# SwiGLU over 8192 rows on one core: loads and stores on one DMA queue in four-row groups, against two-row tiles with the stores on ScalarE's queue

## The chip, the cores and the metric

One of the eight cores of a Trainium2 chip runs the kernel. The metric is the device time of one execution in microseconds (us). Three runs of the kernel before took 938.91, 939.05 and 939.8 us, median 939.05.

A core has five engines that run programs of their own: PE (TensorE, not used here), DVE (VectorE), ACT (ScalarE), POOL (GpSimd) and SP (SyncE, which here only issues DMA transfers). Sixteen DMA engines move data between the main memory (HBM) and the on-chip buffer (SBUF, 128 partitions).

## The reference

The input has 8192 rows of 8192 float32 numbers. Each row has a left half `a` and a right half `b` of 4096 numbers:

```python
a, b = np.split(x, 2, axis=-1)
silu_b = b / (1 + np.exp(-b))
return a * silu_b
```

So 268.44 MB are read, 134.22 MB are written, and each number of the output costs one SiLU and one product.

## The kernel before, in words

There are three buffers, `slot0` to `slot2`, each with 64 KiB in each of the 128 partitions. That is all the room there is: work flows through these three.

The rows go in 16 groups of 512. A partition takes four neighbouring rows of a group. A group is loaded by two transfers (`load`, L61), each with two rows in each partition: 64 KiB in one piece per partition, 8.39 MB in all. Group g has a slot `keep[g]` for its first two rows and a slot `thru[g]` for the other two (L51 to L54). `swiglu` (L72, L74) runs SiLU on ACT in place on `b`, and then the product on DVE. For the first two rows there is one pair of instructions over 128x8192, for the other two a pair of 128x4096 for each row. The products of all four rows are written side by side into `keep[g]`, over numbers that are no longer needed, so that `store` (L81) writes the group in one transfer of 64 KiB per partition.

All transfers are issued by SP, on one queue, in the order that the loop of L88 to L100 writes out: the loads of group g+1 ahead of the store of group g.

```python
load(g + 1, 0)
load(g + 1, 1)
store(g)
```

`load(g + 1, 0)` goes into the slot that the second half of group g has just left, and waits for DVE's last product. `load(g + 1, 1)` goes into the slot from which group g-1 was stored, and waits until that store has landed. `store(g)` waits for DVE's last product of group g. Each engine works through its own instructions in order, so whatever stands behind a waiting instruction waits too.

The kernel writes its schedule by hand: `behind` (L39) tells the framework which of the earlier instructions on a slot a new one has to wait for, and that the others are ordered already.

Of the kernel before, what the change touches and what calls it, by code (L numbers as in the profile page):

```python
# [1 line left out]

# [4 lines left out]

_SILU = mybir.ActivationFunctionType.Silu


@with_exitstack
def kernel(
    ctx: ExitStack,
    tc: tile.TileContext,
    x: bass.AP,
    out: bass.AP,
):

    nc = tc.nc
    N, M = x.shape
    half = M // 2
    P = nc.NUM_PARTITIONS
    R = 4
    ngroups = N // (P * R)

    xv = x.tensor.reshape([N // R, R * M]).ap()  # L30
    ov = out.tensor.reshape([N // R, R * half]).ap()

    pool = ctx.enter_context(tc.tile_pool(name="sbuf", bufs=1))
    ctx.enter_context(tc.manual_schedule())
    slots = [pool.tile([P, 2 * M], x.dtype, name=f"slot{s}") for s in range(3)]
    touched = [[] for _ in slots]
    newest = {}

    def behind(inst, of, *targets):  # L39


        for s in of:
            for t in touched[s]:
                if t not in targets and t is not newest.get(inst.ins.engine):
                    tc.declare_no_dep(inst.ins, t.ins, reason="ordered by the other waits")
        for s in of:
            touched[s].append(inst)
        newest[inst.ins.engine] = inst
        return inst

    keep, thru = [0, 2], [1, 1]  # L51
    for g in range(2, ngroups):
        keep.append(thru[g - 1])
        thru.append(keep[g - 2])  # L54
    free = {}
    landed = {}
    last = {}

    def load(g, second):
        s = (thru if second else keep)[g]  # L60
        inst = nc.sync.dma_start(  # L61
            out=slots[s], in_=xv[g * P : (g + 1) * P, second * 2 * M : (second + 1) * 2 * M]
        )
        behind(inst, [s], *([free[s]] if s in free else []))
        landed[g, second] = inst

    def swiglu(g, second, k0, k1):
        s, o = (thru if second else keep)[g], keep[g]
        rows = slots[s].rearrange("p (k s c) -> p k s c", k=2, s=2)
        a, b = rows[:, k0:k1, 0], rows[:, k0:k1, 1]  # L70
        to = slots[o].rearrange("p (k c) -> p k c", k=R)[:, 2 * second + k0 : 2 * second + k1]
        gate = nc.scalar.activation(out=b, in_=b, func=_SILU)  # L72
        behind(gate, [s], landed[g, second])
        prod = nc.vector.tensor_mul(out=to, in0=a, in1=b)  # L74
        behind(prod, {s, o}, gate, *([last[g]] if g in last else []))
        last[g] = prod
        free[s] = prod

    def store(g):
        s = keep[g]  # L80
        inst = nc.sync.dma_start(out=ov[g * P : (g + 1) * P], in_=slots[s])  # L81
        behind(inst, [s], last[g])
        free[s] = inst

    load(0, 0)
    load(0, 1)
    load(1, 0)
    for g in range(ngroups):  # L88
        swiglu(g, 0, 0, 2)
        for k in range(2):  # L90
            swiglu(g, 1, k, k + 1)
        if g == 0:
            load(1, 1)
            store(0)
        elif g + 1 < ngroups:
            load(g + 1, 0)
            load(g + 1, 1)
            store(g)
        else:
            store(g)  # L100


# [1 line left out]
_INS = ['x']  # L104
_OUTS = [((8192, 4096), 'float32')]


# [23 lines left out]
```

## Time and profile before

| what | value |
|---|---|
| median of three runs | 939.05 us |
| span of the profiled execution, first to last instruction | 936.2 us |
| DMA queue of SP, share of 16 engines' span | 99.6% |
| moved | 402.67 MB, mean 430 GB/s |
| DVE busy | 279.2 us, 48 products |
| ACT busy | 227.7 us, 48 SiLUs and a table load |
| ACT, 128x8192 / 128x4096 | 7.03 / 3.61 us each |
| DVE, 128x8192 / 128x4096 | 8.69 / 4.42 us each |
| ACT waited for loads | 675.5 us |
| DVE waited for ACT | 629.9 us |

The profile gives the span of its one execution and no separate time for it; 936.2 us stand beside the 938.91 to 939.8 us of the three runs.

The page gives busy time for each engine, and then the span in 40 slices, where each digit is a busy share in tenths. The DMA row is the mean over the 16 DMA engines. The chain of waits follows the work back from the last instruction: at each step to what released it. "Another core or an unknown queue" in it is time for which the profile names no releaser. A timeline row has the start in us, the time that it took, engine, line and operation, output and input with their shapes, and in brackets how long the engine was idle before it and what ended that. A DMA transfer is split over the 16 DMA engines, and on each into packets; here a packet is the 64 KiB of one partition, eight packets for each transfer and engine. The trace has a record of each packet with its start, duration and size.

### The profile page before, as it was taken

What the parts mean: (1) busy time and instruction counts of PE and PEld (TensorE: products, weight loads), DVE (VectorE), ACT (ScalarE), POOL (GpSimd) and SP (SyncE); (2) the same over time, 40 slices, a digit from 0 to 9 for tenths busy, and PEclk for the clock granted to TensorE, in tenths of its full rate; (3) what the DMA queues carried; (4) which work ended last, traced back from release to release, by engine and by line L of the source; (5) the groups of instructions that cost most, each with busy time, mean ns of one, the idle gap of its engine ahead of it and who ended that gap; (6) DMA issues with size and microseconds to landing.
All of it is one profiled execution on the core that took longest, in us unless ns stands there. A gap on an engine that the chain in (4) does not pass through costs nothing.

```text
span 936.2 us, 235 instructions
## 1 busy us (share of the span) xinstructions
DVE 279.2 (30%) x48; ACT 227.7 (24%) x49; POOL 0.2 (0%) x4
## 2 busy tenths in 40 slices
DVE  0446033060330603316033160331503315033250
ACT  0433032330323303233032330413304133041330
POOL 0000000000000000000000000000000000000000
DMA  9999999999999999999999999999999999999997
GB/s 403 448 428 423 423 428 448 431 420 448 426 426 445 428 426 437 440 423 437 440 420 440 440 426 431 442 428 423 448 442 414 442 442 417 440 440 412 448 437 344
DMA packets 6914, 402.67 MB, mean 430 GB/s; under 512 B 768, under 2 KB 768, under 8 KB 768
## 3 DMA queue, kind: packets, MB, share of 16 engines
q1 hardware_dynamic: 6912, 402.66, 99.6%
q14 instruction: 2, 0.02, 0.0%
HBM read 268.44 MB, written 134.22 MB: 430 GB/s over the span
## 4 chain that ended last, share of the span: by engine, by line
DMA 67%; DVE 14%; another core or an unknown queue 9%; ACT 6%; SPq 1%; DVEq 0%; issue 0%
DMA slot<-in_x_dram 62%; DVE slot L74 14%; ACT slot L72 6%; DMA out_dram<-slot 5%; SPq L61 1%; DVEq L126 0%
## 5 line engine op out<-in xcount | busy, mean ns | idle before, releaser
L74 DVE TENSOR_TENSOR slot<-slot 128x4096 f32<-128x4096 f32 (+1 forms) x48 | 279.2, 5845 | 629.9 <-ACT slot L72 629.9
L72 ACT ACTIVATE slot<-slot 128x4096 f32<-128x4096 f32 (+1 forms) x48 | 226.4, 4748 | 675.5 <-DMA slot<-in_x_dram 675.5
L72 ACT ACT_TABLE_LOAD x1 | 1.3, 1283 | 0.7 <-PEq L115 0.7
L115 POOL MEMSET const-bfloat16-1.0<- 128x1 bf16 x1 | 0.1, 102 | 0.0
L115 POOL MEMSET const-uint8-127<- 128x1 uint8 x1 | 0.1, 102 | 0.0
L115 POOL MEMSET const-float32-0.0<- 128x1 f32 x1 | 0.1, 99 | 0.2 <-issue 0.2
L115 POOL MEMSET const-float32-1.0<- 128x1 f32 x1 | 0.1, 99 | 0.0
## 6 DMA issues: line engine op xcount, KB each, us to landing
slot<-in_x_dram SPq DMA_DIRECT2D x32, 32.8
out_dram<-slot SPq DMA_DIRECT2D x16, 57.7
```

The costliest lines, as they stand in the source:

```text
L61: inst = nc.sync.dma_start(out=slots[s], in_=xv[g * P : (g + 1) * P, second * 2 * M : (second + 1) * 2 * M])
L72: gate = nc.scalar.activation(out=b, in_=b, func=_SILU)
L74: prod = nc.vector.tensor_mul(out=to, in0=a, in1=b)
L115: nc = _bacc.Bacc("TRN2", target_bir_lowering=False, num_devices=1)
```

## The change

The slots stay. What flows through them is cut in another way:

- The rows go in 33 tiles: the first and the last have one row in each partition (128 rows, 4.19 MB to load), the 31 between have two (256 rows, 8.39 MB). Tile i has slot i mod 3, for its input and its products.
- A load still is 64 KiB per partition (32 KiB for the two one-row tiles), and still is issued by SP. `load(i + 3)` waits until the store of tile i has landed.
- A store is 32 KiB per partition (16 KiB for the one-row tiles). Stores 0 to 29 are issued by ACT, on its own queue, each right behind the tile's SiLU; of these, 17 and 19 are issued by POOL. Stores 30, 31 and 32 are issued by SP, behind the last load.
- SiLU and product run over both rows at once (128x8192), except in tile 0 (two pieces of 128x2048), tile 31 (row by row) and tile 32 (its one row).

On the engines: DVE has 35 products for 48, ACT 35 SiLUs and 28 stores for 48 SiLUs, POOL two stores, SP 33 loads and 3 stores for 32 loads and 16 stores.

The core of the diff:

```diff
-    R = 4
-    ngroups = N // (P * R)
+    rows = [1] + [2] * (N // (2 * P) - 1) + [1]
+    first = [P * sum(rows[:i]) for i in range(len(rows))]
+    last = len(rows) - 1
...
+    def load(i):
+        s, r = i % 3, rows[i]
+        src = x[first[i] : first[i] + P * r].rearrange("(p r) m -> p (r m)", r=r)
+        inst = nc.sync.dma_start(out=slots[s][:, : r * M], in_=src)
+        behind(inst, s, *([stored[i - 3]] if i >= 3 else []))
+        landed[i] = inst
...
+    def swiglu(i, k0, k1, c0, c1):
+        s, r = i % 3, rows[i]
+        v = slots[s][:, : r * M].rearrange("p (k s c) -> p k s c", k=r, s=2)
+        to = slots[s][:, : r * half].rearrange("p (k c) -> p k c", k=r)
+        b = v[:, k0:k1, 1, c0:c1]
+        gate = nc.scalar.activation(out=b, in_=b, func=_SILU)
+        behind(gate, s, landed[i])
+        prod = nc.vector.tensor_mul(out=to[:, k0:k1, c0:c1], in0=v[:, k0:k1, 0, c0:c1], in1=b)
+        behind(prod, s, gate, *([made[i]] if i in made else []))
+        made[i] = prod
...
+    def store(i, engine):
+        s, r = i % 3, rows[i]
+        dst = out[first[i] : first[i] + P * r].rearrange("(p r) m -> p (r m)", r=r)
+        inst = engine.dma_start(out=dst, in_=slots[s][:, : r * half])
+        behind(inst, s, made[i])
+        stored[i] = inst
...
-    for g in range(ngroups):
-        swiglu(g, 0, 0, 2)
-        for k in range(2):
-            swiglu(g, 1, k, k + 1)
-        if g == 0:
-            load(1, 1)
-            store(0)
-        elif g + 1 < ngroups:
-            load(g + 1, 0)
-            load(g + 1, 1)
-            store(g)
+    for i in range(3):
+        load(i)
+    for i in range(last + 1):
+        if i == 0:
+            swiglu(i, 0, 1, 0, half // 2)
+            swiglu(i, 0, 1, half // 2, half)
+        elif i == last - 1:
+            swiglu(i, 0, 1, 0, half)
+            swiglu(i, 1, 2, 0, half)
         else:
-            store(g)
+            swiglu(i, 0, rows[i], 0, half)
+        if i < last - 2:
+            store(i, nc.gpsimd if i in (17, 19) else nc.scalar)
+            load(i + 3)
+        else:
+            store(i, nc.sync)
```

More of the change, by code (lines that the diff above doesn't have):

```diff
@@ L26 @@
     P = nc.NUM_PARTITIONS
-    R = 4
-    ngroups = N // (P * R)
-    xv = x.tensor.reshape([N // R, R * M]).ap()
-    ov = out.tensor.reshape([N // R, R * half]).ap()
+    rows = [1] + [2] * (N // (2 * P) - 1) + [1]
+    first = [P * sum(rows[:i]) for i in range(len(rows))]
+    last = len(rows) - 1
     pool = ctx.enter_context(tc.tile_pool(name="sbuf", bufs=1))
@@ L37, with behind @@
     newest = {}
[L39 to L47, printed above, removed]
+    landed, made, stored = {}, {}, {}
+    def behind(inst, s, *targets):
+        for t in touched[s]:
+            if t not in targets and t is not newest.get(inst.ins.engine):
+                tc.declare_no_dep(inst.ins, t.ins, reason="ordered by the other waits")
+        touched[s].append(inst)
@@ L48, in behind @@
         newest[inst.ins.engine] = inst
         return inst
[L51 to L87, printed above, removed]
-    for g in range(ngroups):
-        swiglu(g, 0, 0, 2)
-        for k in range(2):
-            swiglu(g, 1, k, k + 1)
-        if g == 0:
-            load(1, 1)
-            store(0)
-        elif g + 1 < ngroups:
-            load(g + 1, 0)
-            load(g + 1, 1)
-            store(g)
-        else:
-            store(g)
+    def load(i):
[4 more added lines that the diff above has]
+        landed[i] = inst
```

## The prediction

> **What bounds the kernel now.** I read the page first: the engines' busy shares, the digits of the slices, the queues. Then the chain of waits, then the timeline, and last the records of single DMA packets.
>
> ```profile
> DVE 279.2 (30%) x48; ACT 227.7 (24%) x49; POOL 0.2 (0%) x4
> ...
> DMA  9999999999999999999999999999999999999997
> ...
> q1 hardware_dynamic: 6912, 402.66, 99.6%
> ```
>
> No engine is busy a third of the span, while the one DMA queue fills 99.6% of it, 9 in every slice but the last. So the kernel is bound by moving 402.66 MB, and waits on ACT, DVE or SP matter only where they leave the DMA engines nothing to do. The chain shows no such place:
>
> ```profile
> 609.68 8.77 DVE slot L74 x2
> 618.45 0.02 issue
> 618.47 0.33 SPq L61
> 618.80 6.57 another core or an unknown queue
> 625.37 0.02 issue
> 625.39 38.61 DMA slot<-in_x_dram
> ```
>
> The 6.57 us are the rest of the store before: the load issued at 618.47 is queued behind it. A transfer is always in the queue.
>
> The packet records give the price of the stream. Each of the 16 DMA engines moves 384 packets of 64 KiB. A packet is recorded with 2418 ns (the median; records overlap by about 4 ns, so 2414 ns from start to start), load or store alike. For one engine, on the mean: first packet at 1.86, 0.76 more on the first packet, 384 x 2.414 = 926.98, 47 borders between transfers at about 6 ns = 0.27, 2.53 at switches from load to store, 0.28 elsewhere: 932.7 us. The records end at 932.8 on the mean and at 935.02 on the slowest engine, 2.24 later; 0.38 more to the landing and 0.81 to the end of the span make 936.2. The three times shown have the median 939.05, so 2.85 us lie outside the span; I keep them.
>
> What is left to gain is the 2.53 us and the spread of 2.24. Where the 2.53 come from is seen in the timeline, since ACT starts 0.02 us after a load lands:
>
> ```profile
> 22.54 7.03 ACT L72 ACTIVATE slot<-slot 128x8192 f32<-128x8192 f32 x1 [20.53 <-DMA slot<-in_x_dram]
> ...
> 41.89 7.12 ACT L72 ACTIVATE slot<-slot 128x4096 f32<-128x4096 f32 x2 [12.32 <-DMA slot<-in_x_dram]
> ...
> 61.24 7.03 ACT L72 ACTIVATE slot<-slot 128x8192 f32<-128x8192 f32 x1 [12.23 <-DMA slot<-in_x_dram]
> ...
> 81.43 7.12 ACT L72 ACTIVATE slot<-slot 128x4096 f32<-128x4096 f32 x2 [13.16 <-DMA slot<-in_x_dram]
> ...
> 818.86 7.03 ACT L72 ACTIVATE slot<-slot 128x8192 f32<-128x8192 f32 x1 [31.56 <-DMA slot<-in_x_dram]
> ...
> 838.74 7.12 ACT L72 ACTIVATE slot<-slot 128x4096 f32<-128x4096 f32 x2 [12.85 <-DMA slot<-in_x_dram]
> ...
> 877.49 7.03 ACT L72 ACTIVATE slot<-slot 128x8192 f32<-128x8192 f32 x1 [31.63 <-DMA slot<-in_x_dram]
> ...
> 896.77 7.12 ACT L72 ACTIVATE slot<-slot 128x4096 f32<-128x4096 f32 x2 [12.26 <-DMA slot<-in_x_dram]
> ```
>
> A load behind a load lands 19.35 us later (22.54, 41.89, 61.24). The load that has the first store behind it takes 20.19 (61.24 to 81.43), a late one 19.88 (818.86 to 838.74), the last one 19.28. The packet records put the excess into the load's last packet before a store, engine by engine: 0.91 us on the mean at the first switch, 0.116 on the mean of the other fourteen, 0.063 on the mean of the last five (3, 56, 15, 241 and 2 ns), with a median of 0.010 there. Switches from store to load cost 0.005. This small stall is what the change multiplies.
>
> **The change, part by part.**
>
> Bytes: the same. Packets per engine: loads 31 x 8 of 64 KiB and 2 x 8 of 32 KiB, stores 31 x 8 of 32 KiB and 2 x 8 of 16 KiB, 528 for 384. No row shows a 32 KiB packet; 8 KiB instruction fetches during the run took 309 and 311 ns (307 at the least), which beside 2418 for 64 KiB leaves some 5.4 ns per packet: 144 x 5.4 = 0.78 us, between 0 and 1.2. Borders: 65 x 6 ns = 0.37 for 0.27.
>
> Stores on ACT's queue: issuing one took SP 0.43 us at the median. On ACT it waits for DVE's product (8.69 us for two rows), and behind it stands the next ACTIVATE. That needs a load that lands one tile later: a two-row tile moves 8.39 + 4.19 MB, 8 x (2.414 + 1.21) = 29.0 us, and ACT 7.03 plus DVE 8.69 end 15.8 after a landing. So 13 us cover the wait, and it costs nothing; the ACT chain would have to double first.
>
> Slots: load i+3 waits for store i to land. If the two queues take turns packet by packet, store i is issued 16 us after load i lands and lasts 29, done at 45 to 47; load i+2 lands at 58. SP's queue still holds a load for some 11 us when the next arrives. I cost it at 0. Were loads always served first, the load queue would empty and the stores then have the engines alone; a count of the queues by these rows leaves about 1.4 us without work, so 0 to 1.4.
>
> The stores of tiles 17 and 19 go through POOL, which issues no DMA in the trace of before. From below the 0.43 of SP; from above the 11 us of slack hide it, and only what exceeds them would show, twice. I take 0.
>
> First tile: half the bytes, landing near 12.5 instead of 22.5; the loads behind it keep the engines full either way, so 0. Last tiles: the last load (4.19 MB) is followed on SP's queue by stores 30 and 31, 9.7 us each; its ACT 3.61 and DVE 4.42 are over 8.1 us after landing, 11 us before store 31 is through. 0, as now, where the last DVE work lies under the store before.
>
> Taking turns: today there are 15 switches from load to store per engine. With both queues full and turns by packet, each of 240 store packets of tiles 0 to 29 follows a load packet, and one more switch comes at the end: 241. Price of one: 0 from below (nothing excludes that a second queue lets an engine read ahead past the stall, and below 0 is excluded because packets already run back to back), 0.91 from above, the first switch, with all engines within 0.5 us of each other. The nearest rows are the late switches, when the engines have drifted 3.5 us apart, as they will under turns. Between their median 0.010 and their mean 0.063 I take 0.037: 241 x 0.037 = 8.9 us in place of 2.53.
>
> The Trainium skill, page "DMA: Bandwidth & Descriptors", section "Issuing engines are not separate DMA queues", has it that DMAs of several engines share the same 16 DMA engines, so a second queue saves only issue time. By it alone the sum would be that of the first rival below. No run here shows two such queues yet.
>
> Sum for the mean engine: 1.86 + 0.76 + 926.98 + 0.78 + 0.37 + 0.28 + 8.9 = 939.9; the slowest 2.24 later, 942.2; landing and end 1.19: span 943.4; with 2.85 outside: **946 us**, 0.7% slower.
>
> **The rivals.**
>
> 1. Faster: the switch is free with two queues. What speaks for it: a load's last packet waits where the one queue turns; with two, the other queue's packets are already fetched, and three of the last five switches cost 15 ns or less. Against: 241 chances for a stall in place of 15. Sum without stalls: 931.0 + 0.28 of spread (the engines' after the first load) + 1.19 = 932.5, that is 935.4 us, 0.4% faster. It decides below about 7 ns a switch; from 7 to 23 the time is within the band.
>
> 2. Turns by whole transfers: an engine takes the eight packets of one DMA before it looks at the other queue. Then there are some 33 switches: at 0.063 to 0.116 each 2.1 to 3.8 us, span 936.5 to 938.3, 939.4 to 941.1 us, at the middle 940.2: hardly a change. For it: turns are seen nowhere in this trace. The same page, section "Queues, rings and completion order", has engines go round between queues by packets of about 9 to 17 descriptors, which comes nearest to this rival if one of this trace's records is one descriptor.
>
> 3. The full price: each switch costs the mean of the fourteen, 0.116: 28.0 us, span 962.4, 965.3 us. For it: turns come before engines settle, and most switches before 600 us cost 0.1 to 0.23. At 0.91 each it would be some 219 us more; all engines in step 241 times is what the drift speaks against.
>
> 4. The change doesn't do what it says: the two queues don't overlap, because ACT's store waits hold up the next ACTIVATE or POOL's issue is late, and the engines run dry. The 11 to 13 us of cover speak against it; a miss of 1 us per tile would be 33 us.
>
> **How the numbers follow.** Forecast (0.02 to 0.09 a switch, 942 to 959 us) 0.40; rival 1 0.27; rival 2 0.15; rival 3 0.13; rival 4 and the rest 0.05. About 0.2%, 1.9 us, is what a measurement of this kernel can tell from no change: the band is 937.2 to 940.9. Faster 0.26 (nearly all of rival 1), same 0.16 (most of rival 2 and the edges of the others), slower 0.58. The range goes from 934.5, under rival 1 with its packet price at 0, to 966, over rival 3. Above lie 0.91 a switch and rival 4, below hardly anything: at 2.414 a packet the stream alone needs 927.
>
> **What would show it.** Two hardware queues on the page, about two thirds of the share on SP's and one third on ACT's; stores that last about 29 us from issue to landing if turns go by packet, nearer 10 to 20 if by whole transfers. ACT would still wait for loads, some 13 us a tile, not for DVE. 64 KiB packets still at 2418 ns, with the switch's price on those before a store: under 7 ns is rival 1, about 37 the forecast, 116 rival 3. A DMA share below 99% with gaps is rival 4. Wrong altogether would be a packet that takes longer all through because reads and writes of HBM run at once: the trace of before has them side by side for only 0.5 to 3.5 us at each switch, and there the other packets keep their 2418.

## The result, and the profile after

The changed kernel takes 935.07 us (median of four runs, 934.9 to 935.77), the kernel before 939.25 beside it (938.91 to 939.8): ratio 0.9961 [0.9949, 0.9973]. The forecast was 946 us, slower. The first rival, a free switch between two queues, had 935.4 us.

The profiled execution took 935.77 us, the longest of the four, and its span is 934.0; before it was 936.2. The page, in the order in which it was read before:

```profile
DVE 278.5 (30%) x35; ACT 226.6 (24%) x36; POOL 1.4 (0%) x6
...
DMA  9999999999999999999999999999999999999998
...
q1 hardware_dynamic: 5184, 278.92, 69.1%
q10 hardware_dynamic: 4032, 115.35, 28.6%
q0 software_dynamic: 288, 8.39, 2.1%
```

Nothing has changed in what bounds the kernel: the DMA engines are full in every slice but the last, and the engines' work is what it was. The traffic now comes from three queues: q1 is SP's (all loads and the last three stores), q10 is ACT's, q0 POOL's with its two stores.

The chain of waits around the place shown of before:

```profile
590.93 8.70 DVE slot L56
599.63 0.02 issue
599.65 32.70 DMA out_dram<-slot
632.36 0.01 issue
632.37 38.50 DMA slot<-in_x_dram
```

It now goes from product to store, from store to the load that takes its slot, and from there to SiLU. Stores are on the path because they last long: the page's list of DMA issues (issue to landing, median us, in the last column) has

```profile
out_dram<-slot ACTq DMA_DIRECT2D x27, 4096.0 KB, 36.3
...
out_dram<-slot POOLq DMA_DIRECT2D x2, 4096.0 KB, 33.0
```

That is the sign named for turns by packet: 8 x (2.414 + 1.21) = 29 us of turns, and the rest is waiting behind the store before.

The timeline, where ACT's SiLU starts 0.02 us after its load lands:

```profile
815.87 7.03 ACT L54 ACTIVATE slot<-slot 128x8192 f32<-128x8192 f32 x1 [21.95 <-DMA slot<-in_x_dram]
831.65 0.34 ACTq L63 DMA_DIRECT2D out_dram<-slot  x1
844.88 7.03 ACT L54 ACTIVATE slot<-slot 128x8192 f32<-128x8192 f32 x1 [21.98 <-DMA slot<-in_x_dram]
860.67 0.34 ACTq L63 DMA_DIRECT2D out_dram<-slot  x1
873.88 7.03 ACT L54 ACTIVATE slot<-slot 128x8192 f32<-128x8192 f32 x1 [21.97 <-DMA slot<-in_x_dram]
```

A tile passes every 29.0 us (844.88, 873.88), which is the bare price of 8 load and 8 store packets taking turns: nothing is lost at the switches. ACT issues a store 15.8 us after the tile's load landed and is then 12.9 us (861.01 to 873.88) ahead of its next work.

The packet records say it directly. Take for each size the usual duration (2418 ns for 64 KiB, 1213 for 32, 611 for 16) and call what a packet takes beyond it its **stall**. On the mean of the 16 engines:

| stalls in us per engine | before | after |
|---|---|---|
| first packet of all | 0.75 | 0.57 |
| first store | 0.92 | 0.77 |
| all later switches from load to store | 1.64 (14 switches) | 0.11 (some 203 switches) |
| elsewhere | 0.36 | 0.01 |
| sum | 3.67 | 1.46 |
| slowest engine behind the mean | 2.2 | 1.1 |

After the first store there are 188.6 switches per engine from a load's packet to one on ACT's queue, 0.6 ns each on the mean, and 14 to one on POOL's, 0.0. The stalls give back 2.2 us and the spread 1.0; the smaller packets with their borders cost some 0.75, and the first packet starts 0.25 later: 2.2 us, as by the spans. The medians differ by 4.2. Of the other 2.0 us, 0.7 is there because the profiled execution of after is its longest (the three others have spans of 933.1 to 933.4). Between time and span lie 1.8 us in after and 1.7 to 2.3, mostly 2.1, in the runs of before whose spans are known: that is 0.3 more. The last 0.95 is an estimate: 939.25 less 2.1 is a span of 937.15 for the median execution of before, and the profiled one has 936.2. So the table explains a little over half of the gain; where the longer executions of before lose their time, no trace shows.

### The profile page after: what moved, and what is told of

Read it like the earlier page. It is cut to its first block, busy times and chain, and to the rows that moved or that the text cites. A ratio compares the mean times of both kernels' runs of the same rounds, so it can differ in the third digit from the quotient of the medians.

```text
span 934.0 us, 215 instructions
## 1 busy us (share of the span) xinstructions
DVE 278.5 (30%) x35; ACT 226.6 (24%) x36; POOL 1.4 (0%) x6
## 3 DMA queue, kind: packets, MB, share of 16 engines
q0 software_dynamic: 288, 8.39, 2.1%
## 4 chain that ended last, share of the span: by engine, by line
DMA 78%; DVE 11%; ACT 9%; another core or an unknown queue 1%; issue 0%; SPq 0%; ACTq 0%
DMA slot<-in_x_dram 40%; DMA out_dram<-slot 37%; DVE slot L56 11%; ACT slot L54 9%; SPq L45 0%; ACTq L63 0%
## 5 line engine op out<-in xcount | busy, mean ns | idle before, releaser
L56 DVE TENSOR_TENSOR slot<-slot 128x8192 f32<-128x8192 f32 (+2 forms) x35 | 278.5, 7960 | 638.5 <-ACT slot L54 638.4
L54 ACT ACTIVATE slot<-slot 128x8192 f32<-128x8192 f32 (+2 forms) x35 | 225.3, 6443 | 685.2 <-DMA slot<-in_x_dram 685.2
## 6 DMA issues: line engine op xcount, KB each, us to landing
out_dram<-slot ACTq DMA_DIRECT2D x27, 4096.0 KB, 36.3
```

The lines of the kernel that those rows point to most:

```text
L56: prod = nc.vector.tensor_mul(out=to[:, k0:k1, c0:c1], in0=v[:, k0:k1, 0, c0:c1], in1=b)
```

## The experiments

Three theories at the start. **Two queues** (Q in the expectations): a load's last packet is held up when a store follows it on the same queue, and not when the store comes from another; the gain is the arrangement of the queues. **Store size** (P in the expectations): the smaller and more frequent stores are what takes the stalls away, on whatever queue. **Tail and POOL**: the gain is made at the end, by the last three stores on SP, or by the two stores on POOL. Later ones, on what starts a stall, stand ahead of the runs that test them. All edits are against the changed kernel. Each run has the kernel before beside it on the same chip, and the ratio is to that; as the chips differ, the ratio is the safer number between runs.

**one_queue**: all stores go to SP's queue.

```diff
-            store(i, nc.gpsimd if i in (17, 19) else nc.scalar)
-            load(i + 3)
+            store(i, nc.sync)
...
+        if 1 <= i <= last - 2:
+            load(i + 2)
```

> The changed kernel's tiles and sizes, but every store goes on SP's queue, each behind the load of two tiles later: 32 switches from load to store per DMA engine, all inside one queue. Theory Q (a load's last packet is held up when the next packet on the same queue is a store, and a second queue hides that): 0.9 us at the first switch and about 0.1 at each of the other 31, some 4 us of stalls per engine, the slowest engine about 2 us behind the mean, 938 to 940 us. Theory P (what stalled was the store of 64 KiB packets in blocks of 8.39 MB; 32 KiB stores do not stall in any queue): 935 us, with hardly a stall after the first store.

939.79 us, 1.0022 [1.0013, 1.003]. So without the second queue the gain is gone, and more. The stalls are 3.2 us per engine: 1.0 at the first store, 0.049 on the mean at each of the next 29, fading after 620 us. But this order has a fault of its own: the last load stands behind store 30, and the last store waits up to 5.3 us for its product: 4.0 us of gaps per engine. So the loss is not the queue's alone. The kernel one_queue_tail mends that.

**one_queue_tail**: one queue, with the last load ahead of the last three stores.

```diff
-        if i < last - 2:
-            store(i, nc.gpsimd if i in (17, 19) else nc.scalar)
-            load(i + 3)
-        else:
-            store(i, nc.sync)
+        store(i, nc.sync)
+        if 1 <= i <= last - 3:
+            load(i + 2)
+        if i == last - 3:
+            load(last)
```

> All stores on SP's queue as in the first one-queue run, but with the last load ahead of the last three stores, as the changed kernel has it; in the first one-queue run the last store waited up to 5 us for its product. Theory Q (the stall belongs to switches inside one queue): 2.5 to 3 us of stalls as there, the wait at the end gone, 1.000 of the kernel before, within 0.001. Theory P (smaller stores do not stall): 0.996.

940.23 us, 1.0019 [1.0006, 1.0032], with no gap at the end. Theory Q's 1.000 is missed by a little, theory P's 0.996 by far. The wait at the end is gone, but no time is won by it, since the engines, which in one_queue end within 0.2 us of their mean, end further apart here. Its page shows one queue, and the same full DMA row but for the last slice:

```profile
span 938.3 us, 213 instructions
...
DMA  9999999999999999999999999999999999999997
...
q1 hardware_dynamic: 9504, 402.66, 99.6%
```

Same tiles, same packets, same bytes; 4.3 us more span than after, and 5.1 us more by the medians on one chip (after_again, next, has 935.18). The records account for it: 3.96 us of stalls per engine for 1.46 (0.89 at the first store, 0.079 on the mean at the 29 later ones, single ones up to 0.95), and the slowest engine is 3.1 us behind the mean for 1.1. 2.5 and 2.0 make 4.5. Store size falls; two queues stands. But the 0.079 is a mean of very unequal switches: the 13 up to store 14 take 2.15 us per engine, the last 16 together 0.12, or 7 ns each. A switch inside one queue can stall, and need not. The engines drift apart meanwhile, from 0.45 us between the first and the last of the 16 at the first store to about 3 from store 14 on; they do in before, too. Whether that ends the stalls no run shows; after has none at its second and third store, with the engines 0.35 us apart. Against the kernel before, the finer tiles on one queue lose 2.1 us of span, so the second queue earns 4.3 and the tiles give back half of it.

**after_again**: the changed kernel once more, on the chip of one_queue_tail, no edit.

> The changed kernel as it is, so that it stands beside the other runs on one chip. All theories: 0.995 to 0.997 of the kernel before; stalls of about 1.5 us per engine, nearly all at the first store.

935.18 us, 0.9965 [0.9953, 0.9978], stalls 1.75 us per engine for 1.46: the result repeats.

**no_pool**, and **no_pool_again** on another chip: stores 17 and 19 go to ACT's queue as well.

```diff
-            store(i, nc.gpsimd if i in (17, 19) else nc.scalar)
+            store(i, nc.scalar)
```

> The changed kernel with stores 17 and 19 on ACT's queue too, none on POOL. The step of the prediction that priced POOL's two stores at nothing: the same time, 935 us, within 0.5. If the two POOL stores brought the gain (theory E, the gain is in the side edits), 937 us or more.

> The run without POOL's two stores once more, for a second profile: does the stall of 1.4 us per engine at the last load, ahead of the first store on SP's queue, come back? If it is a property of this order: 1 us or more there again, 0.998 to 1.000 of the kernel before. If it was chance: no stall there and 0.996 to 0.997.

937.35 us, 0.9992 [0.9983, 1.0001], and 937.29, 0.9985 [0.9975, 0.9994]. With the last three stores on SP's queue, two stores out of 33 carry most of the gain, which was not expected. (The changed kernel did not run on the chip of no_pool; tail_on_act, which differs from it only in the queue of the last three stores, took 934.95 us there.) The stream is as free of stalls as after's up to the very end; there the last load's packets, which store 30 follows on SP's queue, stall for 1.40 and 1.20 us per engine. The timeline of no_pool at the end:

```profile
866.89 29.37 SPq L45 DMA_DIRECT2D slot<-in_x_dram  x2
871.97 7.03 ACT L54 ACTIVATE slot<-slot 128x8192 f32<-128x8192 f32 x1 [21.95 <-DMA slot<-in_x_dram]
...
898.53 7.12 ACT L54 ACTIVATE slot<-slot 128x4096 f32<-128x4096 f32 x2 [19.53 <-DMA slot<-in_x_dram]
...
910.14 3.62 ACT L54 ACTIVATE slot<-slot 128x4096 f32<-128x4096 f32 x1 [4.49 <-DMA slot<-in_x_dram]
```

The same place in after:

```profile
864.66 29.33 SPq L45 DMA_DIRECT2D slot<-in_x_dram  x2
...
899.22 7.12 ACT L54 ACTIVATE slot<-slot 128x4096 f32<-128x4096 f32 x2 [18.31 <-DMA slot<-in_x_dram]
...
908.93 3.62 ACT L54 ACTIVATE slot<-slot 128x4096 f32<-128x4096 f32 x1 [2.59 <-DMA slot<-in_x_dram]
```

The last load is one row, 8 x 1.213 = 9.7 us. In after it lands 9.71 us behind the load before (899.22 to 908.93), here 11.61. It is issued later, too: at 895.94, when the load before it lands in 2.6 us; in after at 893.66, 5.5 us ahead. Call this its lead. The chain shown of after says why it is later. The load waits for store 29 to land, and a store on ACT's queue waits behind the store before: 36.3 us at the median up to tile 17. A store on POOL's queue has no store ahead of it, and from tile 19 on all stores land after about 33 us. In no_pool the median is 37.6 over the whole run. The runs of no_pool spread over 936.01 to 938.61 us; that would fit a stall that differs from execution to execution, but only the two profiled ones have traces.

**late_pool**: if that reading holds, two later tiles should do as well.

```diff
-            store(i, nc.gpsimd if i in (17, 19) else nc.scalar)
+            store(i, nc.gpsimd if i in (27, 29) else nc.scalar)
```

> The changed kernel with the two POOL stores moved from tiles 17 and 19 to 27 and 29. Without POOL's stores the last load was issued only 2.6 us before the load ahead of it landed, and 1.0 to 1.2 us of stalls stood at the first store behind it; with them 5.5 us before, and none. If what POOL's stores do is to let a store go beside another on a third queue, and so to land the later stores 3 to 4 us earlier: the same here, no stall at the last load, 0.996 to 0.997 of the kernel before. If it is where they stand in the run that matters: a stall there, 0.998 to 0.999.

935.13 us, 0.9974 [0.9965, 0.9983]: the gain is back, though one of its eleven runs took 938.13 us, which lies among no_pool's. The timeline of its end:

```profile
860.31 0.53 POOL L63 DMA_DIRECT2D out_dram<-slot  x1 [58.96 <-DVE slot L56]
864.22 29.44 SPq L45 DMA_DIRECT2D slot<-in_x_dram  x2
...
898.45 7.12 ACT L54 ACTIVATE slot<-slot 128x4096 f32<-128x4096 f32 x2 [18.34 <-DMA slot<-in_x_dram]
...
908.15 3.62 ACT L54 ACTIVATE slot<-slot 128x4096 f32<-128x4096 f32 x1 [2.58 <-DMA slot<-in_x_dram]
```

The last load is issued at 893.33, 5.1 us ahead, and lands 9.70 us behind the one before: no stall.

**tail_on_act** and **no_pool_tail_act**: the last three stores on ACT's queue, with and without POOL's two.

```diff
-            store(i, nc.sync)
+            store(i, nc.scalar)
```

> The changed kernel with the last three stores on ACT's queue in place of SP's: they then take turns with the last loads. If the order at the end brings nothing: 935 us. If the last load, kept back by store 29 and 30, makes the last store wait for its product, the end comes some 3 to 8 us later, 938 to 943 us: the last load would land later by the half of what the stores take from it, with 8.1 us of ACT and DVE behind it and only a part of store 31 to cover them.

> No store on POOL and the last three stores on ACT's queue: loads on SP, every store on ACT. In the run without POOL, 1.4 us of stalls per engine stood at the last load ahead of the first store on SP's queue. If that switch inside SP's queue is all that the run without POOL lost: 0.996 to 0.997 of the kernel before, as the changed kernel. If POOL's two stores do something for the stream itself: 0.999, as the run without POOL.

934.95 us, 0.9969 [0.9956, 0.9981], and 936.0, 0.9973 [0.996, 0.9986]. With POOL's stores the place of the last three is worth nothing that can be told (0.23 us of mean gap at the end). Without them the stall at the last load is gone, and 1.28 us of gap stand in its place, in which the last store waits for its product. No store follows the last load on its queue there; but it is also issued 4.7 us ahead (895.98 for a landing at 900.64), so queue and lead are not told apart. Between no_pool and no_pool_tail_act the intervals overlap, so by time alone the two are not told apart; by the records they are.

**even_tiles**: 32 tiles of two rows, no one-row tiles at the ends; POOL's stores stay.

```diff
-    rows = [1] + [2] * (N // (2 * P) - 1) + [1]
+    rows = [2] * (N // (2 * P))
...
-            swiglu(i, 0, 1, 0, half // 2)
-            swiglu(i, 0, 1, half // 2, half)
-        elif i == last - 1:
+            swiglu(i, 0, 2, 0, half // 2)
+            swiglu(i, 0, 2, half // 2, half)
+        elif i == last:
```

> The changed kernel with 32 tiles of two rows, no one-row tile at either end; the last tile is computed row by row. The first and last tiles were priced at nothing, since the DMA engines are full either way: 935 us, within 0.5. Theory E (the small ends bring the gain): 937 to 939 us.

936.33 us, 0.9979 [0.997, 0.9987], between the two forecasts and some 1.2 us above the changed kernel's medians. The first store, now at 42 us and twice as long, stalls 1.49 us per engine for 0.77, which is 0.7 of it; the rest no trace shows. The end costs nothing.

What starts a stall? A fixed price for each switch within a queue was the plainest answer; two kernels cut the transfers so that one queue has twice the switches.

**one_queue_halves**: each transfer as two of 64 partitions each.

```diff
+        for h in parts:
+            q = slice(h * P // 2, (h + 1) * P // 2)
+            inst = nc.sync.dma_start(out=slots[s][q, : r * M], in_=src[q])
...
+            for h in range(2):
+                store(i, (h,))
+                load(i + 2, (h,))
```

> One queue, with each load and store cut into two transfers of 64 partitions, taking turns: some 64 switches from load to store in place of 32, and half the pause between stores (8 us for 17). Theory Q with a price per switch (0.05 us each in the one-queue run, 0.9 the first): about 4 us of stalls per engine, 1.6 more than with 32. Theory W (what costs is a store that begins after a pause in the stores: 0.116 us after 39 us in the kernel before, 0.05 after 17 us; the two queues never pause): 8 us of pause cost 0.02 or less, 2 us of stalls per engine, time 1 us under the one-queue run with the mended tail.

1594.1 us (1432.32 to 1599.46): no answer, since something else came first. The page of its 1432.32 us execution:

```profile
GB/s 205 205 222 280 251 315 273 315 294 306 342 275 291 312 256 314 310 281 293 314 289 294 314 278 268 280 283 299 271 280 304 243 313 295 274 292 259 291 260 218
...
q1 hardware_dynamic: 10560, 402.66, 98.2%
```

In the first two slices, in which no store moves yet, the rate is 205 GB/s for the 404 of after, with the queue full: these loads over 64 partitions go at half the rate. Why, no run here shows.

**one_queue_rows**: each transfer as its two rows, over all 128 partitions.

```diff
+        for k in parts:
+            if k < r:
+                inst = nc.sync.dma_start(out=slots[s][:, k * M : (k + 1) * M], in_=src[:, k * M : (k + 1) * M])
...
+            for k in range(2):
+                store(i, (k,))
+                load(i + 2, (k,))
```

> One queue with the mended tail, each load and store of a two-row tile cut into its two rows: packets of 32 and 16 KiB, some 63 switches from load to store per engine in place of 32, pauses of about 8 us between stores in place of 17. The smaller packets and added borders alone cost about 2.6 us (1213 and 611 ns for a half and a quarter of 2418, 64 borders of 6 ns). Theory Q with a price per switch (0.08 us in the one-queue run with the mended tail): 5 us of stalls per engine in place of 4. Theory W: 2 us or less, most of it at the start and the first store.

941.15 us, 1.0031 [1.0018, 1.0043]. About 60 switches, and stalls of 2.7 us per engine for 3.96: 0.85 around the first store, and 1.2 in all after it, where one_queue_tail has 2.3 with half the switches. At 0.079 each it would be 4.6 after the first store. There is no fixed price for a switch. What the time loses here it loses to more packets and borders.

Two theories were left: that the stall comes back after every long pause of the store's queue (W), or only at the first store and after a queue has run dry (D). The next four kernels leave out a part of the output, which gives the stores long pauses; their times are no measure of the change.

**sparse_two** and **sparse_one** store every third tile only, on ACT's queue or on SP's.

```diff
-        behind(inst, s, *([stored[i - 3]] if i >= 3 else []))
+        behind(inst, s, *([stored.get(i - 3) or made[i - 3]] if i >= 3 else []))
...
+        if i % 3 == 0:
+            store(i, nc.scalar)
```

> Leaves out two thirds of the output: only the tiles 0, 3, 6, ... 30 are stored, 11 stores, all on ACT's queue; every tile is loaded and computed. The stores pause for some 39 us each time, as in the kernel before. Theory Q (the stall belongs to a store behind a load inside one queue): no stalls after the first store. Theory W (it belongs to a store that begins after a pause in the stores): about 0.1 us per engine at each of the ten later stores, on the packets of loads around their start.

> Leaves out the same two thirds of the output, but the 11 stores are on SP's queue between the loads; they pause for some 58 us. Both theories: 0.9 us at the first store and about 0.1 us or more per engine at each of the ten later ones. It stands beside the run with two queues: the same bytes and tiles, the queue of the stores alone differs. If it shows no stalls either, the sparse pair tells nothing.

In sparse_two every store from the third on starts with 0.7 to 1.1 us of stall per engine, on a queue of its own, so a second queue alone does not abolish the stall, and two queues in its plain form falls. But in this kernel SP waited for a store ahead of further loads and its queue ran dry in every round, 19 us of gaps per engine in all. The page's DMA row shows it:

```profile
DMA  9999998999899999999999999899999989999994
```

The second store, with some 52 us of pause but no dry queue before it, has 0.07. In sparse_one the first two stores stall 1.08 and 0.41 us (before the second the queue had been dry for 1.8 us); the later ones 0.00 to 0.14, and up to 0.8 on the way back to the load.

**fed_two** and **fed_one** take the dry queue away: only the first row of tiles 1, 4, 7 and so on is stored, and loads go row by row so that always one is queued.

```diff
+        for k in range(r):
+            inst = nc.sync.dma_start(out=slots[s][:, k * M : (k + 1) * M], in_=src[:, k * M : (k + 1) * M])
...
+        if i % 3 == 1:
+            store(i, nc.scalar)
```

> Leaves out five sixths of the output: only the first row of the tiles 1, 4, 7, ... 31 is stored, in 16 KiB packets on ACT's queue; every tile is loaded, row by row in 32 KiB packets, and computed. The stores pause for some 45 us, and the load queue always has a load waiting, which it had not in the sparse run with two queues: there each store began with 0.7 to 1.1 us of stall per engine, but SP's queue had run dry 40 us before. Theory W (a store stream that begins again after a pause stalls, whatever its queue): 0.1 to 1 us per engine at each of the ten later stores. Theory D (it stalls once after the engines' queues have run dry or been started, and hardly otherwise): 0.8 us at the first store, nearly nothing at the ten later ones.

> Leaves out the same five sixths of the output, with the stores on SP's queue between the loads. Theory W and theory D: 0.9 us at the first store; at the ten later ones about 0.1 us or less per engine, as in the other one-queue runs. Against the run with two queues it says what the queue alone does at the same pause and with a load always waiting.

In fed_two the DMA row is nines up to the last slice. The first store stalls 0.53 us per engine; the ten later ones, after pauses of 35 to 50 us, 6 to 11 ns. W falls, and D stands, for two queues. In fed_one the first has 0.18 for the 0.9 expected, and 0.08 behind it, the later ones 7 to 15 ns and 2 to 59 ns on the way back: small, but not as clean. So a pause, one queue, and even the two together are not enough for a stall.

## Why the prediction was wrong, point by point

**The step that failed is "Taking turns": "241 x 0.037 = 8.9 us in place of 2.53".** The mechanism of the turns was right, packet by packet, and their number nearly (some 210 per engine for 241, since about 30 store packets follow a store packet). The price was 0.6 ns, not 37. It had been read off the only switches that the trace of before had, and those lie within one queue, behind a load in the same queue. one_queue_tail shows that it did not carry over: the same tiles on one queue stall 0.079 us on the mean of 29 switches. It wasn't a price of one switch even there, as the last 16 of these show with 7 ns each, and one_queue_rows with twice the switches and less stall. A median of 10 ns beside a mean of 63 had said so: a price of a switch would be near its median, and this was a rare event. Rival 1 had the right price, and its 935.4 us lie 0.3 from the measured median. Its reason, that the other queue's packets are already fetched, no run shows or excludes. Most of its agreement is earned (span 932.5, measured 933.1 to 934.0), part is luck: it left out the first store's 0.77 and took 0.28 of spread where after has 1.1, and it took 2.85 us outside the span where after has 1.8.

The sentence weighed of the Trainium skill, "DMA: Bandwidth & Descriptors", section "Issuing engines are not separate DMA queues", says that all queues share the 16 engines and that a second one saves only issue time. The trace agrees with the first half: the three queues' packets follow each other in the same 16 streams of records. With the second it does not: two queues saved 5.1 us against one, and the one queue left no gap (0.02 us per engine) in which the engines waited for an issue. "By it alone the sum would be that of the first rival" does not follow from it either: if only issue time were saved, the stalls would stay. The section "Queues, rings and completion order" of the same page of the Trainium skill gave rival 2 its turns by 9 to 17 descriptors. Here they go by single records of 64 and 32 KiB; how many descriptors a record is, no run shows.

**"I take 0" for POOL's stores** was wrong as to what they do, not as to what they cost. Their issue of 0.53 to 0.67 us is hidden, as forecast. But they let the stores, which ran 7 us behind on ACT's queue, catch up by 3 to 4 us, and without them most of the gain is lost at the last load.

**"SP's queue still holds a load for some 11 us"** failed in size for the same reason. Stores were put at 29 us and last 33 to 36, so that at the last load but one 9.2 us are left with POOL's two (864.66 to 873.88 in after) and 5.1 without (866.89 to 871.97 in no_pool). At the last load it is still less, 5.5 and 2.6: the load ahead of it lands 25 and 27 us behind its forerunner, and not 29 (873.88 to 899.22 in after), as store 30 no longer takes turns with it.

**"0" for the one-row tiles** missed a term of about 1.2 us (even_tiles), of which the smaller stall at the smaller and earlier first store is 0.7. At the end they were worth nothing, as forecast.

**2.85 us outside the span** was about 1 too large. It paired the span of one execution with the median of others.

Right were: what bounds the kernel; the packets' price (1213 and 611 ns, so 4 and 6.5 ns above the shares of 2418); ACT's waits at nothing, with 12.9 us of cover for 13; no starving of the engines (rival 4); the tail. The forecast that ACT would wait some 13 us a tile for loads cannot be read off the page as it stands: it shows 22, since it counts the store's 8.7 us wait for DVE as idle too.

**Left open.** Why the first store, and a store after a dry queue, stalls 0.2 to 1.5 us per engine. Whether it is the nearly dry queue that makes the last load stall in no_pool: it goes with 2.6 and 2.4 us of lead and is absent at 5 and more four times (after, after_again, late_pool, even_tiles), but the lead was not varied alone. And why single engines stall at switches within a queue, and in before, one_queue and one_queue_tail less and less as the run goes on.

## What to carry to other kernels

A stall seen in a trace is a price of the place where it was seen: before it is multiplied, ask whether the new place has the same condition (here, both directions in one queue), and look at median beside mean. Where the DMA engines are full and one core both reads and writes, loads and stores on two queues that never run dry ran here without any loss at switches. The end of the run counts too: with two stores on a third queue the last load was issued 2 us earlier and did not stall, and without them most of the gain was lost; that the lead is the reason is likely, but not shown.

## What the runs showed of the hardware that had not been expected

- Loads over 64 partitions moved 205 GB/s where those over 128 move 404, with a full queue (one_queue_halves).
- With loads and stores of 64 and 32 KiB taking turns on two queues, packets keep the 2418 and 1213 ns that they have alone: reading and writing HBM at once cost nothing extra here, at 431 GB/s.
- The first store's stall isn't at its first packet alone: with the one-row first tile it is 0.2 us in the load packet just ahead of it and 0.55 in the third load packet after that, in after, no_pool and late_pool alike.
